# The two mixers' planner: when an item may reserve, when a bank counts as free, and new planned lengths for gate, convolution and memory

## The chip, the cores and the metric

The kernel runs on one core of a Trainium2 chip. The metric is the device time of one execution in microseconds; the time before is the median of three executions. A core has a matrix engine (PE, with its weight loads shown apart as PEld), a vector engine (DVE), a scalar engine (ACT), a general engine (POOL) and a queue engine (SP). SP and POOL start the transfers. Each engine works through its instructions in the order in which they were written for it, and waits where an instruction needs something that isn't there yet.

## The reference, cut to what matters

It is a two-layer encoder over 512 tokens of width 1024, all in f32, with a memory of 256 tokens:

```python
for layer in range(2):
    xn = rms_norm(x, mix_norm[layer])
    if layer == 0:
        mixed = fox_diff_mixer(xn, ...)     # 8 forgetting heads + 4 differential heads
    else:
        mixed = mlstm_mixer(xn, ...)        # 4 heads, chunkwise in the reference
    x = x + mixed
    x = x + memory_cross_attention(rms_norm(x, ...), rms_norm(mem, ...), wq, wkv, wo)
    x = x + conv_ffn(rms_norm(x, ...), ...)
return rms_norm(x, final_norm)
```

The first mixer projects the normed x to fq, fk, fv (forgetting attention, head width 64) and dq, dk, dv (differential attention). A forgetting head adds a decay that depends on the distance to the scores, a differential head subtracts one softmax from another (`p1 - lam * p2`) and norms its output; the two results stand side by side before the output product with `w_out`. The second mixer convolves q and k over four tokens, applies SiLU, weighs the scores with gates i and f, divides by a sum, norms each head, multiplies by sigmoid(og) and goes through its output product.

## The kernel before, in words

Activations lie transposed in SBUF: eight tiles x0 to x7 of 128 channels by 512 tokens. An f32 product is made of three passes of a faster format: each operand is split into a high and a low part, and `mm3` (lines 340 to 342) issues high by high, low by high, high by low into one PSUM bank. Weights come as 128x1024 tiles `raw` over SP; ACT casts the high part `wh`, DVE subtracts it to give the low part `wl`. There are three buffers each of raw, wh and wl, so at most three weight tiles are in use at once. A product over 1024 channels is 24 matmuls of 512 columns, or 24 of 256 columns where the 256 memory tokens are multiplied (xk0 to xk3 below). Line 262 is the helper that issues every ACT and DVE instruction, so those rows of the profile are told apart by the tile names.

PSUM has four banks "acc" for products, two "s" for scores and norms, two "w" for transposes and weighted sums.

The stages, by the trace: first mixer 0 to about 225 us, its memory attention to about 335, its feed-forward to about 700, second mixer to about 935, then memory attention, feed-forward and the last norm. Within the two mixers (and the memory attention) a small planner, `Plan`, decides the order in which the instructions are written. The code adds items: `take` and `free` name resources (banks, buffers), `dur` is the time on PE, `chain` lists what follows on A (ACT), D (DVE) or as a plain delay ("-"), `prio` ranks, `after` is an earliest planned time, `order` and `deps` are items that must come first. `Plan.run` keeps a planned clock t, goes through the items by rank and issues the first whose time has come; the item's function then writes its instructions. An item of higher rank that is not yet due reserves its resources (`held`), so that items of lower rank that want the same are passed over. `pick.ready` is t after the chain: items that depend on it wait until then in the plan. A low-ranked group of products stands ready as fill: in the first mixer the keys of the memory (xk) and the output product (wo).

Names in the first mixer: `x0` to `x7` also hold softmax rows while their x lies in DRAM, and are loaded again before the residual add. A differential head is weighed by line 793 (`pt` transposed probabilities, `v` values), squared into `tb`, summed by the matmul of line 499, made into `z` on DVE, into `y` on POOL, sent by POOL to DRAM (`roots`), and brought back spread over all partitions (`hrb`); DVE then scales `ta` by hrb and splits it to `mh` and `ml`. For a forgetting head, POOL brings the decays (`fb`) and makes a masked bias `tb` from them, which DVE adds to the scores (lines 750 and 751, transposes 781). A pair of forgetting heads is weighed by line 1008. `tb` has two buffers for both uses.

Names in the second mixer: mqk0 to mqk7 are the products of q (0 to 3) and k (4 to 7), mv the values, mog the output gates. `gates` makes the rows of i and f; `ucols` (line 1630) transposes them to columns; `most` and `emts` spread rows by matmul (line 690) for head 0, `both` by DMA for the others. `score` is line 1721, `dens` lines 1743 and 1744; num and hrb are the numerators and the spread norm of a head.

Of the kernel before, what the change touches and what calls it, by code (L numbers as in the profile page):

```python
# [30 lines left out]
ROW_DMA, SPREAD_DMA, LATE = 2.7, 6.0, 12.0  # L31
# [50 lines left out]


class Plan:

# [9 lines left out]

    def add(self, fn, dur=0.0, deps=(), prio=None, take=(), free=(), chain=(), pre=(), after=0.0, order=(), load=(), st=None):
        it = Item(fn, dur, [d for d in deps if d is not None], len(self.items) if prio is None else prio, take, free, chain, pre, after, order, load, st)
        it.n = len(self.items)
        self.items.append(it)
        return it  # L100

    def run(self):
        todo = sorted(self.items, key=lambda i: (i.prio, i.n))
        eng, t = self.eng, self.t
        while todo:
            soon, pick = float("inf"), None
            held = set()
            for i in todo:
                if any(d.ready is None for d in i.deps + i.order) or held & set(i.take):
                    continue  # L110
                held |= set(i.take)
                if any(len(self.res[r]) < i.take.count(r) for r in i.take):
                    continue
                at = max([i.after] + [d.ready for d in i.deps] + [sorted(self.res[r])[i.take.count(r) - 1] for r in i.take])
                if at <= t:
                    pick = i
                    break
                soon = min(soon, at)
# [14 lines left out]
            t += pick.dur  # L133
            u = t + (0.1 if pick.chain else 0.0)
            for e, d in pick.chain:
                if e == "-":
                    u += d
                    continue
                u = max(u, eng[e]) + d
                eng[e] = u  # L140
                u += 0.06
            for e, d in pick.load:
                eng[e] = max(eng[e], t) + d
            pick.ready = u
            pick.fn()
            for r in pick.free:
                if r == "acc":
                    self.banks[pick.st["banks"].pop(0)] = u
                else:
                    self.res[r].append(u)  # L150
# [138 lines left out]
class Builder:  # L289
# [64 lines left out]
    def p_proj(self, pl, src, xs, evac, chain, deps=(), kdeps=None, edeps=(), prio=None, n=SEQ, nk=KB8, order=None, etake=(), per=2, eorder=(), load=()):  # L354
# [5 lines left out]
        for c, e in zip(cuts, cuts[1:] + [nk]):  # L360
# [18 lines left out]
            )  # L379
        return pl.add(lambda: evac(st["ps"]), 0, [last, *edeps], prio, take=etake, free=("acc",), chain=chain, order=eorder, load=load, st=st)  # L380

# [648 lines left out]
    def p_memory(self, pl, layer, at, step, order=()):  # L1030
# [14 lines left out]
        for c in range(2):  # L1045
            last = pl.add(lambda c=c: load(c), 0, (), 0, after=at + step * c - 10.0, order=[*order, last])
        done = {}
# [552 lines left out]
    def mix1(self):  # L1600
        nc, t, tc = self.nc, self.t, self.tc
        H = 4
        with tc.tile_pool(name="mix1", bufs=1, reuse_waits="tile") as mp:
# [382 lines left out]
```

## Time and profile before

| what | value |
|---|---|
| median of three executions | 1425.62 us (1424.94 to 1427.39) |
| the profiled execution | 1423.48 us |
| its span in the trace | 1421.7 us |
| mean granted PE clock | 0.998 |
| PE busy | 1403.3 us, 99% |
| DVE busy | 1133.5 us, 80% |
| ACT busy | 823.8 us, 58% |
| POOL busy | 129.9 us, 9% |

Between the span and the time of the execution lie 1.8 us. PE is busy in 99% of the span: what a change of order alone can win is the rest, and any time in which PE runs at less than its pace. The view of waits says what PE waited for, the table of windows says in which stage; a time in a window is to be read against the window's length.

### The profile page before, as it was taken

Reading aid. Unit: us, or ns where it says so; the run is one execution under the profiler, and the core shown is the slowest. Engines: PE = TensorE matmul, PEld = TensorE weight load, DVE = VectorE, ACT = ScalarE, POOL = GpSimd, SP = SyncE. Lnnn points to the kernel's source line nnn. Section 1 sums busy time; section 2 is a strip of 40 time slices with the busy share of each in tenths; the row PEclk is TensorE's granted clock in tenths of the full one; section 3 lists DMA queues with packets and bytes.
Section 4 is the critical chain, followed back from the end, with each engine's and each line's share of the span. In section 5 each row is a group of like instructions: output and inputs, shape, how many; then the busy total and the mean of one; then the engine's idle time right before and its main releaser. Section 6 shows DMA issues by size and latency. Waiting matters only on the chain.

```text
span 1421.7 us, 22241 instructions
## 1 busy us (share of the span) xinstructions
PE 1403.3 (99%) x8440; PEld 1262.9 (89%) x8440; DVE 1133.5 (80%) x1906; ACT 823.8 (58%) x1382; POOL 129.9 (9%) x189
## 2 busy tenths in 40 slices
PE   9999999999999999999999999999999999999998
PEld 7878788899889999999887788989988999999997
DVE  7778596666689999999768657667667999999984
ACT  7777574444476656566456654445445665656655
POOL 0001240000001111110001210000000111111000
PEclk9999999999999999999999999999999999999999
DMA  5233224323248777773233322323323886777522
GB/s 205 90 108 108 90 79 152 132 76 133 86 150 217 191 180 184 182 182 106 86 105 112 105 95 97 119 92 120 130 74 120 212 202 171 193 179 185 143 77 80
DMA packets 69211, 190.02 MB, mean 134 GB/s; under 512 B 7552, under 2 KB 7552, under 8 KB 69104
## 3 DMA queue, kind: packets, MB, share of 16 engines
q1 hardware_dynamic: 55648, 153.48, 32.3%
q0 software_dynamic: 12448, 34.00, 13.7%
q8 instruction: 66, 1.08, 0.3%
q10 hardware_dynamic: 1008, 1.12, 0.2%
q14 instruction: 41, 0.34, 0.1%
HBM read 186.43 MB, written 2.15 MB: 133 GB/s over the span
## 4 chain that ended last, share of the span: by engine, by line
PE 83%; DVE 8%; ACT 4%; issue 3%; DMA 1%; POOL 1%; SPq 0%; POOLq 0%; DVEq 0%; ACTq 0%
PE acc L340 16%; PE acc L341 16%; PE acc L342 16%; PE w L340 5%; PE w L342 5%; PE w L341 5%; PE s L340 3%; PE s L341 3%; PE s L342 3%; PE acc L402 2%; PE acc L404 2%; PE acc L403 2%; DVE wl L262 2%; DVE x L262 1%; PE w L1765 1%
## 5 line engine op out<-in xcount | busy, mean ns | idle before, releaser
L262 ACT CAST wh<-raw 128x1024 fp32r<-128x1024 f32 (+2 forms) x229 | 235.0, 1027 | 205.6 <-PE acc L341 118.8
L262 DVE TENSOR_TENSOR wl<-raw,wh 128x1024 fp32r<-128x1024 f32 (+2 forms) x229 | 274.2, 1198 | 38.7 <-ACT wh L262 38.2
L340 PE MATMUL acc<-xh,wh 128*128 128x512 f32 (+1 forms) x800 | 278.6, 348 | 0.8 <-ACT v L262 0.8
L341 PE MATMUL acc<-xl,wh 128*128 128x512 f32 (+1 forms) x800 | 274.0, 343 | 0.0
L342 PE MATMUL acc<-xh,wl 128*128 128x512 f32 (+1 forms) x800 | 273.6, 342 | 0.0
L340 PEld LDWEIGHTS acc<-xh,wh 128*128 128x128 f32 x800 | 152.5, 191 | 14.5 <-ACT v L262 1.2
L342 PEld LDWEIGHTS acc<-xh,wl 128*128 128x128 f32 x800 | 152.4, 190 | 13.9
L341 PEld LDWEIGHTS acc<-xl,wh 128*128 128x128 f32 x800 | 152.5, 191 | 13.2
L262 DVE SCALAR_TENSOR_TENSOR c<-hs,vec,c 128x512 f32<-128x512 f32 x176 | 131.8, 749 | 3.8 <-ACT c L262 0.8
L340 PE MATMUL w<-ah,wh 128*128 128x512 f32 x304 | 115.7, 381 | 0.2 <-ACT c L262 0.2
L342 PE MATMUL w<-ah,wl 128*128 128x512 f32 x304 | 115.2, 379 | 0.0
L341 PE MATMUL w<-al,wh 128*128 128x512 f32 x304 | 115.2, 379 | 0.0
L262 ACT ACTIVATE c<-hs,vec 128x512 f32<-128x512 f32 x88 | 70.8, 811 | 9.9 <-DVE hs L262 5.4
L262 ACT CAST ah<-c 128x512 fp32r<-128x512 f32 x44 | 27.2, 619 | 83.8 <-DVE c L262 83.8
L262 DVE TENSOR_TENSOR x<-acc,x 128x512 f32<-128x512 f32 (+1 forms) x43 | 28.1, 653 | 54.2 <-PE acc L342 53.4
L340 PEld LDWEIGHTS w<-ah,wh 128*128 128x128 f32 x304 | 57.6, 190 | 8.0 <-DVE x L262 0.9
L342 PEld LDWEIGHTS w<-ah,wl 128*128 128x128 f32 x304 | 57.5, 189 | 8.1
L341 PEld LDWEIGHTS w<-al,wh 128*128 128x128 f32 x304 | 57.6, 190 | 6.5
L342 PE MATMUL acc<-mem,wl 128*128 128x256 f32 (+1 forms) x192 | 59.9, 312 | 0.0
L340 PE MATMUL acc<-mem,wh 128*128 128x256 f32 (+1 forms) x192 | 59.6, 311 | 0.0
L341 PE MATMUL acc<-mem,wh 128*128 128x256 f32 (+1 forms) x192 | 59.6, 311 | 0.0
L1446 POOL DMA_DIRECT2D sa<-in_up_dram x36 | 30.8, 857 | 290.6 <-DMA sa<-in_up_dram 212.7
(357 smaller groups left out, 3750.5 us busy)
## 6 DMA issues: line engine op xcount, KB each, us to landing
raw<-in_up_dram SPq DMA_DIRECT2D x52, 512.0 KB, 3.7
sa<-in_up_dram SPq DMA_DIRECT2D x36, 512.0 KB, 3.4
sa<-in_up_dram POOLq DMA_DIRECT2D x36, 512.0 KB, 5.9
raw<-in_down_dram SPq DMA_DIRECT2D x32, 512.0 KB, 3.6
ra<-in_up_dram SPq DMA_DIRECT2D x36, 256.0 KB, 4.0
sb<-in_up_dram POOLq DMA_DIRECT2D x36, 256.0 KB, 4.9
raw<-in_xk_dram SPq DMA_DIRECT2D x16, 512.0 KB, 3.2
raw<-in_wo_dram SPq DMA_DIRECT2D x16, 512.0 KB, 3.3
```

The costliest lines, as they stand in the source:

```text
L262: i = issue(*a, **k)
L340: mm(out, wh, xh, start=first, stop=False, skip_group_check=parts)
L341: mm(out, wh, xl, start=False, stop=False, skip_group_check=parts)
L342: mm(out, wl, xh, start=False, stop=last, skip_group_check=parts)
L402: mm(ps, xh[k][:, ts], wh, start=(k == 0), stop=False)
L403: mm(ps, xh[k][:, ts], wl, start=False, stop=False)
L404: mm(ps, xl[k][:, ts], wh, start=False, stop=(k == 7))
L1446: return add("POOL", 0.0029 * cols, lambda: nc.gpsimd.dma_start(out(), src(), accum_op=ALU.add), deps, due, (), (), 6.0)
L1765: nc.tensor.matmul(ps[:, lo:], vv[s][:, c], a[:], start=(s == 0), stop=(s == 3))
```

## The change

Five things change, none of them in what is computed; the numbers of matmuls, transposes, splits and transfers stay the same.

- A constant `HOLD = 2.5`: an item that is known to be due more than 2.5 us later than the planned clock no longer reserves what it takes, so that lower-ranked items may use it meanwhile.
- The PSUM bank of a channel-major product (`p_proj`) counts as free after the first step of the chain that reads it, where it counted as free at the chain's end (`soon=True`).
- The two transfers of the memory are planned 16 us ahead of their use, 10 before.
- In the second mixer the chain from the gates to `ucols` is a delay of 14 us with loads of 5 on ACT and 7 on DVE (it was 1.0, 7.0 and 0.5 in sequence), the chain to `gk` one of 4 us with loads, `most` and `emts` of head 0 also depend on `gk`, and `both` counts two transfers one after the other.
- The planned chain of the convolution, `cc`, is longer (ACT 0.7, 0.6, 0.6 for 0.52 each, DVE 2.3 for 1.98).

```diff
+HOLD = 2.5
     def add(...):
-        it.n = len(self.items)
+        it.n, it.soon = len(self.items), soon
...
-                held |= set(i.take)
                 if any(len(self.res[r]) < i.take.count(r) for r in i.take):
+                    held |= set(i.take)
                     continue
                 at = max([i.after] + [d.ready for d in i.deps] + [sorted(self.res[r])[i.take.count(r) - 1] for r in i.take])
+                if at < t + HOLD:
+                    held |= set(i.take)
                 if at <= t:
                     pick = i
                     break
...
             u = t + (0.1 if pick.chain else 0.0)
+            clear = None
             for e, d in pick.chain:
...
                 u = max(u, eng[e]) + d
                 eng[e] = u
                 u += 0.06
+                clear = clear or u
...
                 if r == "acc":
-                    self.banks[pick.st["banks"].pop(0)] = u
+                    self.banks[pick.st["banks"].pop(0)] = clear if pick.soon else u
...
-        return pl.add(lambda: evac(st["ps"]), 0, [last, *edeps], prio, take=etake, free=("acc",), chain=chain, order=eorder, load=load, st=st)
+        return pl.add(lambda: evac(st["ps"]), 0, [last, *edeps], prio, take=etake, free=("acc",), chain=chain, order=eorder, load=load, st=st, soon=True)
...
-            last = pl.add(lambda c=c: load(c), 0, (), 0, after=at + step * c - 10.0, order=[*order, last])
+            last = pl.add(lambda c=c: load(c), 0, (), 0, after=at + step * c - 16.0, order=[*order, last])
...
-            g = pl.add(lambda: None, 0, [g], 1, chain=(("A", 1.0), ("D", 7.0), ("A", 0.5)))
-            gk = pl.add(lambda: None, 0, [g], 2, chain=(("-", ROW_DMA),))
+            g = pl.add(lambda: None, 0, [g], 1, chain=(("-", 14.0),), load=(("A", 5.0), ("D", 7.0)))
+            gk = pl.add(lambda: None, 0, [g], 2, chain=(("-", 4.0),), load=(("A", 2.4), ("D", 1.2)))
...
-            cc = (("D", 0.6), ("A", 0.52), ("D", 1.98), ("A", 0.52), ("D", 0.66), ("A", 0.52))
+            cc = (("D", 0.6), ("A", 0.7), ("D", 2.3), ("A", 0.6), ("D", 0.66), ("A", 0.6))
...
-                    b1 = pl.add(most, MM, [uc, qe], p, take=("s",), free=("s",), chain=(("A", 0.5),))
-                    b2 = pl.add(emts, MM, [uc, qe], p + 1, take=("s",), free=("s",), chain=(("A", 0.5),))
+                    b1 = pl.add(most, MM, [uc, gk, qe], p, take=("s",), free=("s",), chain=(("A", 0.5),))
+                    b2 = pl.add(emts, MM, [uc, gk, qe], p + 1, take=("s",), free=("s",), chain=(("A", 0.5),))
                 else:
-                    b1 = b2 = pl.add(both, 0, [uc, gk, *turn[-1:]], p, chain=(("-", SPREAD_DMA),))
+                    b1 = b2 = pl.add(both, 0, [uc, gk, *turn[-1:]], p, chain=(("-", ROW_DMA), ("-", SPREAD_DMA)))
```

The order changes in the two mixers alone: PE's first 329 rows, the memory attentions and the feed-forwards stand as they stood. In the listings below the helper's line is 262 before and 269 after; all lines behind the first edit move by 7.

In the first mixer, the differential heads' norms are issued earlier against the softmax of the forgetting heads. On DVE before, in the softmax of the first pair of forgetting heads (ISA rows add the bias `tb` to scores `s`), the scaling of head 2 by `hrb` stands between two blocks:

```order
L262 TENSOR_SCALAR x_140<-x_140,sm_1507 128x384
L262 COPY pt_1370<-w_1543 128x128
L262 ISA x_142,sm_1557<-s_1550,tb_1551 128x384
L262 ISA sm_1557 128x1
L262 SCALAR_TENSOR_TENSOR ta_1421<-ta_1421,warm,hrb_1568 128x512
L262 ISA x_138,sm_1566<-s_1559,tb_1560 128x512
L262 ISA sm_1566 128x1
L262 RECIPROCAL sm_1557<-sm_1557 128x1
L262 TENSOR_TENSOR ml_135<-ta_1421,mh_129 128x512
```

In the new order the scaling of the same head (`hrb_1400`) stands behind the pair's last block and the splits of kb, 52 rows behind its `z`, where it stood 12 rows behind it:

```order
L269 ISA x_143,sm_1558<-s_1551,tb_1552 128x512
L269 ISA sm_1558 128x1
L269 ISA x_144,sm_1569<-s_1562,tb_1563 128x512
L269 ISA sm_1569 128x1
L269 COPY pt_1408<-w_1571 128x128
L269 COPY pt_1409<-w_1574 128x128
L269 TENSOR_TENSOR kb_115<-tmp_1577,ka_320_1579 64x512
L269 TENSOR_TENSOR kb_117<-tmp_1577,ka_321_1583 64x512
L269 SCALAR_TENSOR_TENSOR ta_1265<-ta_1265,warm,hrb_1400 128x512
L269 TENSOR_SCALAR x_142<-x_142,sm_1499 128x384
```

On POOL, the transfer that brings this hrb stood right behind its roots:

```order
L986 AFFINE_SELECT tb_1501<-fb_1215 128x384
L507 TENSOR_TENSOR y_1486<-z_1485,power 128x4
L448 DMA roots_1532<-y_1486 128x4
L452 DMA hrb_1568<-roots_1532 128x512
L986 AFFINE_SELECT tb_1551<-fb_1217 128x384
L986 AFFINE_SELECT tb_1560<-fb_1215 128x512
```

and now stands behind all eight masks of the pair and the next `fb`:

```order
L455 DMA roots_1363<-y_1324 128x4
L459 DMA hrb_1349<-roots_1327 128x512
L993 AFFINE_SELECT tb_1436<-fb_1312 128x256
L993 AFFINE_SELECT tb_1445<-fb_1314 128x256
L993 AFFINE_SELECT tb_1484<-fb_1312 128x384
L993 AFFINE_SELECT tb_1493<-fb_1314 128x384
L993 AFFINE_SELECT tb_1552<-fb_1312 128x512
L993 AFFINE_SELECT tb_1563<-fb_1314 128x512
L702 DMA fb_1627<-decays_1162 128x512
L459 DMA hrb_1400<-roots_1363 128x512
```

With it, all of head 0's norm comes before the forgetting heads' values; fq0 begins ahead of fv; the scores of differential heads 2 and 3 are written close together among the last of fq0 and the first of fv, and heads 2 and 3 are weighed in the middle of fv3, where they stood in fv2.

At the end of the first mixer, PE before wrote the last weighing (line 1008) with products of the other blocks of wo00 and wo01 around it; xk0 to xk3 had been written among the softmax of the second and third pairs:

```order
L1008 MATMUL w_2425<-pt_2109,v_1213 64x128
L1008 MATMUL w_2425<-pt_2213,v_1213 64x128
L342 MATMUL acc_518_2489<-mh_129,wl_2485 128x512
L340 MATMUL acc_518_2489<-mh_130,wh_2484 128x512
L341 MATMUL acc_518_2489<-ml_136,wh_2484 128x512
L342 MATMUL acc_518_2489<-mh_130,wl_2485 128x512
L340 MATMUL acc_514_2456<-qa_509_2434,wh_2451 128x512
L340 MATMUL acc_518_2489<-mh_125,wh_2484 128x512
L341 MATMUL acc_518_2489<-ml_131,wh_2484 128x512
L341 MATMUL acc_514_2456<-qa_510_2435,wh_2451 128x512
```

Now wo00, wo01 and wo02 are begun among those softmaxes and held until the last weighing, and xk0 follows behind them:

```order
L1015 MATMUL w_2399<-pt_2164,v_1310 64x128
L1015 MATMUL w_2399<-pt_2324,v_1310 64x128
L347 MATMUL acc_375_1843<-qa_507_2408,wh_1838 128x512
L347 MATMUL acc_386_1881<-qa_507_2408,wh_1876 128x512
L347 MATMUL acc_443_2073<-qa_507_2408,wh_2068 128x512
L348 MATMUL acc_375_1843<-qa_508_2409,wh_1838 128x512
L349 MATMUL acc_375_1843<-qa_507_2408,wl_1839 128x512
L348 MATMUL acc_386_1881<-qa_508_2409,wh_1876 128x512
L349 MATMUL acc_386_1881<-qa_507_2408,wl_1877 128x512
L348 MATMUL acc_443_2073<-qa_508_2409,wh_2068 128x512
L349 MATMUL acc_443_2073<-qa_507_2408,wl_2069 128x512
L347 MATMUL acc_512_2421<-mem_1518,wh_2416 128x256
```

What moved: four products of 24 matmuls of 256 columns went from before the last weighing to behind it, and 34 more matmuls of wo (63 for 29) from behind it to before it.

In the second mixer, PE before wrote `ucols` right behind the values (mv), ahead of mqk0:

```order
L403 MATMUL acc_1465_7884<-wl_8038,xh_1452_7835 128x512
L404 MATMUL acc_1465_7884<-wh_8037,xl_1453_7836 128x512
L1630 MATMUL s_8074<-ident,cv_7961 128x4 x4
L340 MATMUL acc_1508_8087<-xh_1415_7636,wh_8082 128x512
L341 MATMUL acc_1508_8087<-xl_1416_7637,wh_8082 128x512
L342 MATMUL acc_1508_8087<-xh_1415_7636,wl_8083 128x512
```

Now 21 of mqk0's 24 matmuls come first:

```order
L347 MATMUL acc_1506_8080<-xh_1449_7818,wh_8075 128x512
L348 MATMUL acc_1506_8080<-xl_1450_7819,wh_8075 128x512
L349 MATMUL acc_1506_8080<-xh_1449_7818,wl_8076 128x512
L1637 MATMUL s_8102<-ident,cv_7961 128x4 x4
L347 MATMUL acc_1506_8080<-xh_1452_7835,wh_8075 128x512
L348 MATMUL acc_1506_8080<-xl_1453_7836,wh_8075 128x512
```

Behind it, the spreading of `most` and the first scores move back by six matmuls each, and at the last head the order is `at3`, twelve matmuls of mog, lines 1743 and 1744, where 24 stood between.

More of the change, by code (lines that the diff above doesn't have):

```diff
@@ L94, in __init__, with add @@
         self.res["acc"] = self.banks.values()
-    def add(self, fn, dur=0.0, deps=(), prio=None, take=(), free=(), chain=(), pre=(), after=0.0, order=(), load=(), st=None):
+    def add(self, fn, dur=0.0, deps=(), prio=None, take=(), free=(), chain=(), pre=(), after=0.0, order=(), load=(), st=None, soon=False):
         it = Item(fn, dur, [d for d in deps if d is not None], len(self.items) if prio is None else prio, take, free, chain, pre, after, order, load, st)
-        it.n = len(self.items)
+        it.n, it.soon = len(self.items), soon
         self.items.append(it)
```

## The prediction

> **What bounds the kernel now.** I read the page's busy shares first, then the table of windows over the two mixers, the view of waits, and the timeline around each wait.
>
> ```profile
> PE 1403.3 (99%) x8440; PEld 1262.9 (89%) x8440; DVE 1133.5 (80%) x1906; ACT 823.8 (58%) x1382; POOL 129.9 (9%) x189
> ```
>
> PE is the bound. Of the span of 1421.7 us it is idle for 18.4. The change only reorders two stages, so what counts is their share of that idle time, and any time at less than full clock. In the windows below, the columns are the stretch, its length, then each engine's busy time; the last three are PE's granted clock, the transfers' share and GB/s.
>
> ```profile
> 75.00:100.00 25.00, 24.30 (x119) 20.68 (x118) 20.19 (x60) 17.93 (x40) 2.39 (x4) 1.00 0.36 114
> 100.00:125.00 25.00, 24.01 (x130) 20.45 (x129) 16.77 (x53) 20.45 (x47) 4.97 (x8) 1.00 0.26 84
> 150.00:160.00 10.00, 7.50 (x34) 6.41 (x33) 6.43 (x17) 5.04 (x12) 5.19 (x8) 0.83 0.29 78
> 180.00:200.00 20.00, 18.55 (x136) 16.02 (x136) 19.21 (x65) 15.86 (x39) 9.11 (x15) 1.00 0.19 63
> 740.00:760.00 20.00, 18.53 (x89) 15.97 (x88) 13.63 (x18) 14.87 (x19) 1.13 (x2) 1.00 0.25 79
> 760.00:780.00 20.00, 19.06 (x87) 15.86 (x86) 17.80 (x26) 12.65 (x22) 4.64 (x10) 1.00 0.39 124
> 780.00:800.00 20.00, 19.15 (x83) 14.59 (x82) 14.63 (x29) 12.98 (x22) 5.18 (x9) 1.00 0.49 154
> 850.00:900.00 50.00, 49.69 (x271) 42.76 (x270) 35.77 (x57) 23.16 (x33) 4.45 (x7) 1.00 0.27 90
> ```
>
> So the first mixer loses 0.70 + 0.99 in 75 to 125, 2.50 (with a low clock besides) in 150 to 160, and 1.45 in 180 to 200, where DVE is busy 19.21 of 20: there DVE, not PE, sets the pace. The second loses 1.47 + 0.94 + 0.85 + 0.31. That is 9.2 us and the clock: the change can't win more than about 11 us. PE's longest waits in 75 to 235 us (in all, times, longest) name who ends them:
>
> ```profile
> PE w L781 <- DVE pt L262: 2.5, 1, 2.5
> PE w L793 <- ACT pt L262: 1.0, 1, 1.0
> PE w L781 <- DVE sm L262: 0.9, 1, 0.9
> ```
>
> **First term: the scaling of head 2, -4.2 us.** The longest wait, from the timeline:
>
> ```profile
> 151.11 0.56 POOL L695 DMA_DIRECT2D fb<-decays  x1 [0.30 <-POOL tb L986]
> ...
> 152.19 0.75 DVE L262 SCALAR_TENSOR_TENSOR ta<-ta,warm,hrb 128x512 f32<-128x512 f32 x1 [2.06 <-DMA hrb<-roots]
> ...
> 153.63 0.69 DVE L262 TENSOR_TENSOR ml<-ta,mh 128x512 fp32r<-128x512 f32 x1
> ...
> 154.24 0.77 DVE L262 TENSOR_SCALAR x<-x,sm 128x384 f32<-128x384 f32 x1
> ...
> 155.26 0.69 PE L781 MATMUL w<-ident,x 128*128 128x128 f32 x2 [2.50 <-DVE pt L262]
> ...
> 157.02 0.63 PE L341 MATMUL acc<-xl,wh 128*128 128x512 f32 x1
> 157.45 0.63 PE L342 MATMUL acc<-xh,wl 128*128 128x512 f32 x1
> ...
> 158.72 0.38 PE L342 MATMUL acc<-xh,wl 128*128 128x512 f32 x1
> 158.93 0.38 PE L340 MATMUL acc<-xh,wh 128*128 128x512 f32 x1
> ```
>
> DVE, in order, stands 2.06 us before the spread norm; behind it stand the copy of pt that frees the "w" bank, and PE's transposes behind that: 2.50 us. Then matmuls start 0.43 us apart until 158.72 and 0.21 apart from there (0.216 is used for a 512-column matmul below): 3.46 us at half pace, 1.7 lost. The price of this place is 2.5 + 1.7 = 4.2. The Trainium skill (TensorE: Matmul & The Clock Gate, Part 1) says that the array falls to half its clock after an idle window of about 3.4 us. Here 2.50 us, right behind sums of two columns, was enough, so the measurement decides; by the page's length alone the place would cost 2.5 and the forecast be 1.7 us later.
>
> In the new order this scaling stands behind both last blocks of the pair. Is its hrb there? POOL now issues it behind the pair's last mask, which needs the second-last pair of blocks read, since `tb` has two buffers.
>
> ```profile
> hrb<-roots POOLq DMA_DIRECT2D x7, 256.0 KB, 3.6
> ```
>
> ```profile
> L262 DVE CUSTOM_DVE_ANT_0 x<-s,tb 128x512 f32<-128x512 f32 (+3 forms) x27 | 13.2, 498 | 3.1 <-PE s L751 1.5 <-POOL tb L986 1.3
> L262 DVE TENSOR_TENSOR kb<-tmp,ka 64x512 fp32r<-64x512 f32 x4 | 2.8, 706 | 0.1
> L262 DVE SCALAR_TENSOR_TENSOR ta<-ta,warm,hrb 128x512 f32<-128x512 f32 x2 | 1.5, 749 | 2.1 <-DMA hrb<-roots 2.1
> L262 DVE TENSOR_TENSOR ml<-ta,mh 128x512 fp32r<-128x512 f32 x2 | 1.4, 685 | 0.0
> ```
>
> From that read: a mask of about 0.6 (estimated by the 512-column passes here), 0.30 and 0.56 for fb, then 3.6 to land: some 5.1 us. On DVE meanwhile stand one scaling (0.75), one ml (0.69), one evacuation of the same size (0.69), two kb (1.41), two full-width score blocks (about 0.7 each), and ten short rows (about 1.5): 6.4. So 1.3 us to spare: I take no wait; the other end is the whole 4.2 again. Heads 0, 1 and 3 have 13 us or more of DVE work between z and hrb (their rows summed by such durations), for a path that took head 2 no more than 9.
>
> **Second term: heads 2 and 3 packed, +0.3.** Their 16 score blocks now stand among 47 product matmuls (10.2 us) with 32 score matmuls (5.0) and the transposes (1.3): 16.5 us of PE. DVE's rows for them, from 81 to 122 us before:
>
> ```profile
> L262 DVE CUSTOM_DVE_ANT_0 x<-s,dmask 128x512 f32<-128x512 f32 (+3 forms) x17 | 8.3, 496 | 3.1 <-PE s L751 3.1
> L262 DVE TENSOR_TENSOR wl<-raw,wh 128x1024 fp32r<-128x1024 f32 x5 | 6.0, 1208 | 0.8 <-ACT wh L262 0.8
> L262 DVE SCALAR_TENSOR_TENSOR x<-x,sm,x 128x512 f32<-128x512 f32 (+3 forms) x8 | 4.3, 542 | 1.9 <-ACT x L262 1.8
> ```
>
> 16 x 0.496 + 8 x 0.542 + 4 x 1.208 = 17.1, with some 7.5 for the reciprocals, the copies of pt, the qa and ta that stand between (an estimate by their sizes): 24.6 us. In DVE's queue a row begins before the last one's end (ml above ends at 154.32, the next begins at 154.24): 0.08 each over 71 rows, 5.7 less, some 19 to 20. PE may run two blocks ahead (two "s" banks), about 1.5 us of DVE, and the end of DVE's work falls beside fv1 to fv3, which need none of it. 20 - 1.5 - 16.5 = 2.0 lost, where 1.69 was. The waits of 0.9 and 1.0 (L781 for sm, L793 for pt) go with the old order, since the weighings now stand 10 us behind the scores. Ends for the loss: 0, and 8.1 (no overlap, nothing hidden).
>
> **Third term: the end of the first mixer, +2.2.** The fill among the softmaxes shrinks by 96 x 0.108 (256 columns) - 34 x 0.216 = 3.0 us, and DVE has three splits fewer to make there (3.6 us). They balance. What is new stands behind the last weighing:
>
> ```profile
> 218.44 2.37 PE L1008 MATMUL w<-pt,v 128*64 128x512 f32 x16
> ...
> 220.88 0.59 ACT L262 CAST qa<-w 128x512 fp32r<-128x512 f32 x1 [2.51 <-PE w L1008]
> ...
> 221.51 0.69 DVE L262 TENSOR_TENSOR qa<-w,qa 128x512 fp32r<-128x512 f32 x1 [2.81 <-ACT qa L262]
> ...
> 222.77 1.06 ACT L262 CAST wh<-raw 128x1024 fp32r<-128x1024 f32 x1 [1.30 <-PE acc L341]
> ```
>
> Before, products of other blocks covered the cast of 0.59 and the split of 0.69. Now PE has nothing between: 0.65 lost, then three matmuls (0.65) cover the split. wo00, wo01, wo02 hold all three weight buffers until 1.75, 2.2 and 2.6 us after the weighing. xk0's cast can't start before the first of these: it ends at 3.0 (0.4 lost), and its low part, on DVE behind two residual adds of about 0.7, at 4.5; PE has two matmuls first and loses 1.3. Before the weighing itself, the last block takes about 4.4 us through DVE, ACT, PE and DVE, and PE has 3.8 of work: 0.6. With 0.7 for the masks (POOL now sends head 3's hrb between two of them) it is 3.65, for 1.45 before. Ends: no more than before (DVE is relieved more than the fill shrinks, and xk's parts come in time) and 6.65 (the 3.0 us of missing fill shown whole).
>
> **Fourth term: the second mixer, -1.65.**
>
> ```profile
> 750.68 0.38 PE L1630 MATMUL s<-ident,cv 4*128 4x4 f32 x4 [1.47 <-DVE cv L262]
> ...
> 770.09 0.61 ACT L262 ACTIVATE k<-cv 128x512 f32<-128x512 f32 x1
> 770.75 1.77 PE L1721 MATMUL s<-q,k 128*128 128x512 f32 x4 [0.94 <-ACT k L262]
> ...
> 784.39 1.77 PE L1721 MATMUL s<-q,k 128*128 128x512 f32 x4 [0.85 <-ACT k L262]
> ...
> 860.73 0.75 DVE L262 SCALAR_TENSOR_TENSOR num<-num,vec,hrb 128x512 f32<-128x512 f32 x1 [1.16 <-DMA hrb<-roots]
> ...
> 881.42 0.91 PE L1744 MATMUL w<-mk,ones 128*128 128x384 f32 x2 [0.32 <-DVE mk L262]
> ```
>
> Behind 21 matmuls (4.5 us) ucols waits for nothing: 1.47 won. But ACT's and DVE's queues up to the first k are the old ones, so k is still there at 770.70 and L1721 still starts near 770.75, now with six more matmuls done: 6 x 0.216 = 1.3 is what remains. At head 1 the memory's rows have moved out of the way of k, and the 0.85 goes (ends: all or nothing). At head 3 only 12 matmuls (2.6 us) stand between the last score and L1744, for 24 before, and the scaling by head 2's hrb, which already waited 1.16 us, stands ahead of the sum on DVE: 0.8 for 0.32, +0.5 (ends -0.3 and +1.5). -1.3 - 0.85 + 0.5 = -1.65.
>
> **At nothing.** The memory's earlier transfers: no row of PE waits for them; each holds one of the three raw buffers 6 us longer, and two still carry the stream, as a product of 24 matmuls lasts 5.2 us and loading, cast and split take less than twice that. Banks counted free early: PE still waits for the true read, and no wait of PE on "acc" stands in the list of 75 to 235 us. The larger cc only moves rows.
>
> Sum: -4.2 + 0.3 + 2.2 - 1.65 = -3.35. The profiled execution goes from 1423.48 to 1420.1; the median of 1425.62 is 2.1 above that execution, so 1422.3. A difference of 0.2% (2.85 us) is about what can be told from none.
>
> **Rivals.**
> - The end of the first mixer costs nothing new, because three splits fewer on a DVE that is busy 19.21 of 20 free more than the fill lost: 3.35 + 2.2 = 5.5 won, 1420.1. For it: DVE's share there. Against: the three held buffers.
> - The wait for hrb only moves: head 2's lands after DVE gets there, or head 3's holds up the masks. 2.5 to 4.2 come back: 1424.8 to 1426.5. The spare 1.3 us decides.
> - Slower: the packed heads wait row by row. If each row of DVE waits for ACT's answer, durations add without overlap: 8.1 lost for 1.69, +2.75 in all, 1428.4. The change is slower by more than 0.2% once the stretch loses over 8.2. For it: DVE waited 1.8 us for ACT ahead of its eight combinations there, with more work between them than now.
> - Slower, by the clock alone: short pauses, each under a microsecond, halve PE's pace for much of the 16.5 us; five drops by 1.7 make +8.5 and 1430.8. The window 180 to 200, with 1.45 us of such pauses at a clock of 1.00, speaks against it. This is what the Trainium skill's page TensorE: Matmul & The Clock Gate describes under "A second HAM failure mode: psum-queue depth-cycling"; by that rule the clock would swing here, and this trace doesn't show it.
>
> **How the numbers follow.** Forecast 0.42 (its own range 1419.5 to 1425: 0.27 faster, 0.15 same); first rival 0.17, faster; second 0.17 (0.01 faster, 0.12 same, 0.04 slower, with the end of the mixer at its bad end); third 0.19 (0.04 same, 0.15 slower, since it would delay the heads' norms too); fourth 0.05, slower. Together faster 0.45, same 0.31, slower 0.24. The range runs from the first rival with the packed heads' loss at 0 (1418.1), the second mixer's last head at its good end (1417.3) and 0.8 of the spread between runs (1416.5) to the third with 0.6 of spread (1429).
>
> **What would show it.** In the profile after: PEclk 1.00 throughout the first mixer and no wait of L781 beyond 1 us for pt around 150 us; PE idle about 2 us in the packed stretch (some 80 to 100 us); about 2.4 us of idle in front of xk0, with waits on a cast and on wl; no wait at L1630, one of about 1.3 at the first L1721, none at the second, and about 0.8 at L1744 of the last head. A low clock anywhere in 75 to 230, or a DVE wait for hrb of over 2 us, would make the forecast wrong.

## The result, and the profile after

The changed kernel takes 1428.88 us (median of 18 runs, 1425.31 to 1432.15), the kernel before beside it 1424.96 (18 runs, 1423.66 to 1428.08). The ratio is 1.0026, with a 95% interval of 1.0018 to 1.0034: slower by 0.26%, 3.9 us. The forecast was 1422.3. The time lies at the upper end of its range (1429.0), on the side that had the smallest chance (0.24).

The profiled execution of after took 1431.04 us, with a span of 1429.3. The number of instructions is the same; PE's busy time grew by 4.1 us, its idle time by 3.5. The two profiled executions lie 7.6 us apart, the medians 3.9: the profile of before is one of its quicker executions, that of after one of its slower, so the two profiles show more loss than the medians.

```profile
PE 1407.4 (98%) x8440; PEld 1265.0 (89%) x8440; DVE 1133.3 (79%) x1906; ACT 823.1 (58%) x1382; POOL 129.2 (9%) x189
```

The table of windows of after, as in the prediction (stretch, length, busy times, then PE's granted clock, the transfers' share and GB/s):

```profile
75.00:100.00 25.00, 24.64 (x130) 20.32 (x128) 21.47 (x74) 23.40 (x57) 2.35 (x3) 1.00 0.18 54
100.00:125.00 25.00, 22.93 (x110) 19.01 (x109) 17.71 (x45) 16.84 (x33) 2.42 (x5) 1.00 0.40 138
125.00:150.00 25.00, 24.28 (x117) 21.29 (x118) 18.43 (x49) 18.65 (x40) 9.08 (x15) 0.93 0.35 102
150.00:175.00 25.00, 25.00 (x131) 21.67 (x130) 19.39 (x42) 15.27 (x28) 1.38 (x4) 1.00 0.32 109
175.00:200.00 25.00, 21.75 (x121) 16.24 (x121) 19.57 (x67) 14.96 (x40) 12.53 (x21) 0.93 0.24 64
200.00:225.00 25.00, 22.55 (x132) 17.23 (x131) 17.56 (x57) 13.45 (x32) 3.51 (x7) 1.00 0.28 86
740.00:760.00 20.00, 20.00 (x95) 17.27 (x95) 14.12 (x20) 13.09 (x18) 0.59 (x1) 1.00 0.24 80
850.00:900.00 50.00, 48.09 (x219) 39.08 (x218) 26.34 (x40) 24.12 (x35) 4.50 (x6) 0.97 0.25 80
```

The same windows of before, where the prediction showed other cuts:

```profile
125.00:150.00 25.00, 24.87 (x124) 20.56 (x123) 21.64 (x52) 20.07 (x39) 5.06 (x7) 1.00 0.34 110
150.00:175.00 25.00, 22.50 (x111) 19.37 (x109) 15.46 (x34) 11.52 (x22) 6.15 (x10) 0.93 0.32 100
175.00:200.00 25.00, 23.55 (x172) 19.66 (x172) 21.19 (x70) 17.63 (x42) 10.19 (x17) 1.00 0.16 55
200.00:225.00 25.00, 24.91 (x155) 19.66 (x154) 20.78 (x66) 14.15 (x37) 4.10 (x9) 1.00 0.51 173
```

The stretch of the first term (150 to 175) is what was promised: PE is busy all of it at full clock, where it lost 2.50 us and 7% of the clock. But two stretches that ran at full clock now don't (125 to 150 and 175 to 200), and 100 to 125, 175 to 200 and 200 to 225 lose 2.07, 3.25 and 2.45 us. From 75 to 225 PE's idle time is 8.85 us where it was 5.86, and the clock costs 2 x 0.07 x 25 = 3.5 where it cost 1.75: 4.7 more.

The view of waits of after begins with these (in all, times, longest); the first two aren't in the list of before, and the third was 0.32 there:

```profile
PE w L788 <- DVE x L269: 2.4, 1, 2.4
PE w L788 <- ACT ta L269: 2.0, 1, 2.0
PE w L1751 <- DVE mk L269: 1.9, 1, 1.9
```

**A, at 125 us: a row of the memory's on ACT.** The timeline of after:

```profile
116.84 1.22 DVE L269 TENSOR_TENSOR wl<-raw,wh 128x1024 fp32r<-128x1024 f32 x1
...
118.08 0.33 SPq L1049 DMA_DIRECT2D raw<-in_mem_dram  x1
118.50 0.38 SPq L332 DMA_DIRECT2D raw<-in_fq_dram  x1
...
124.07 0.42 ACT L269 ACTIVATE sqt<-raw 128x256 f32<-128x256 f32 x1 [5.08 <-DMA raw<-in_mem_dram]
...
124.39 0.57 ACT L269 COPY ta<-w 128x512 f32<-128x512 f32 x1
...
125.01 0.55 PE L788 MATMUL w<-ident,x 128*128 128x128 f32 x3 [2.03 <-ACT ta L269]
...
126.27 1.05 PE L506 MATMUL s<-ones,tb 128*128 128x2 f32 x8 [0.70 <-ACT tb L269]
```

The first square of the second memory tile stands on ACT one row ahead of the copy of `ta` (the weighed values of differential head 2) that frees a "w" bank. Heads are counted from 0 here, as with the scaling of head 2; the packed "heads 2 and 3" of the prediction are heads 1 and 2 in this count. The tile that the square reads is issued at 118.08, although planned earlier: it needs one of the three raw buffers, and `wl` on DVE gives one back at 118.06. The tile is there at 124.07, ACT stands 5.08 us, and PE 2.03 and 0.70 behind it; then the clock drops.

**B, at 190 us: the fill is used up.** PE has no product left while DVE splits `qa` and `kb`. **C, at 887 us:** the sum of the last head stands on DVE behind the scaling by head 2's `hrb`. B and C in the timeline:

```profile
187.40 0.90 DVE L269 TENSOR_TENSOR kb<-tmp,ka 64x512 fp32r<-64x512 f32 x1
188.31 0.69 DVE L269 TENSOR_TENSOR qa<-tmp,qa 64x512 fp32r<-64x512 f32 x1
189.01 0.69 DVE L269 TENSOR_TENSOR kb<-tmp,ka 64x512 fp32r<-64x512 f32 x1
...
190.85 0.66 PE L788 MATMUL w<-ident,x 128*128 128x128 f32 x4 [2.45 <-DVE x L269]
...
192.34 1.09 PE L788 MATMUL w<-ident,x 128*128 128x128 f32 x4 [0.47 <-DVE sm L269]
...
885.17 0.75 DVE L269 SCALAR_TENSOR_TENSOR num<-num,vec,hrb 128x512 f32<-128x512 f32 x1 [2.79 <-DMA hrb<-roots]
...
887.04 0.91 PE L1751 MATMUL w<-mk,ones 128*128 128x384 f32 x2 [1.91 <-DVE mk L269]
```

To compare runs by stage, the table of experiments gives two lengths from each profiled execution: "first" runs from the start to the first transpose of the memory attention's probabilities (line 1201 of before), "second" from the last matmul of the gate product (line 637) to the first of the last group of four such transposes. Before, the starts stand in these rows (min, median and max duration, first and last start; the last group of four begins 0.33 us ahead of the last start):

```profile
L1201 PE MATMUL w<-ident,xe x64: 272/273/273, 282.9 to 1048.4; 128*128 128x128 f32 x64
```

```profile
L637 PE MATMUL w<-xh,wh x16: 379/379/379, 6.7 to 726.6; 128*40 128x512 f32 x8, 128*100 128x512 f32 x8
```

### The profile page after: what moved, and what is told of

It is laid out like the page before. It is cut to its first block, busy times and chain, and to the rows that moved or that the text cites. A ratio compares the mean times of both kernels' runs of the same rounds, so it can differ in the third digit from the quotient of the medians.

```text
span 1429.3 us, 22252 instructions
## 1 busy us (share of the span) xinstructions
PE 1407.4 (98%) x8440; PEld 1265.0 (89%) x8440; DVE 1133.3 (79%) x1906; ACT 823.1 (58%) x1382; POOL 129.2 (9%) x189
## 3 DMA queue, kind: packets, MB, share of 16 engines
q10 hardware_dynamic: 1008, 1.12, 0.2%
## 4 chain that ended last, share of the span: by engine, by line
PE 83%; DVE 8%; ACT 3%; issue 2%; DMA 2%; POOL 1%; SPq 0%; POOLq 0%; DVEq 0%; ACTq 0%
PE acc L347 17%; PE acc L349 16%; PE acc L348 16%; PE w L347 5%; PE w L349 5%; PE w L348 5%; PE s L347 3%; PE s L349 3%; PE s L348 3%; PE acc L409 2%; PE acc L410 2%; PE acc L411 2%; DVE wl L269 2%; DVE c L269 1%; PE w L1772 1%
## 5 line engine op out<-in xcount | busy, mean ns | idle before, releaser
L349 PEld LDWEIGHTS acc<-xh,wl 128*128 128x128 f32 x800 | 152.8, 191 | 14.0
```

Source lines behind the costliest of these rows:

```text
L349: mm(out, wl, xh, start=False, stop=last, skip_group_check=parts)
```

## The experiments

| kernel | median us (runs) | ratio to before, 95% | first | second |
|---|---|---|---|---|
| before | 1424.96 (18) | | 282.90 | 321.47 |
| after | 1428.88 (18) | 1.0026 (1.0018 to 1.0034) | 287.40 | 323.97 |
| after again | 1428.97 (7) | 1.0040 (1.0025 to 1.0055) | 286.12 | 322.02 |
| first mixer new, second old | 1429.74 (10) | 1.0037 (1.0023 to 1.0050) | 285.25 | 321.73 |
| first mixer old, second new | 1424.27 (11) | 0.9999 (0.9991 to 1.0008) | 282.79 | 324.14 |
| after, sum first | 1429.44 (5) | 1.0032 (1.0020 to 1.0044) | 289.34 | 320.08 |
| after, memory's lead 10 | 1422.20 (11) | 0.9992 (0.9983 to 1.0000) | 279.88 | 321.84 |
| after, fill from 180 | 1426.49 (12) | 1.0023 (1.0014 to 1.0032) | 284.29 | 322.23 |
| first mixer old, second new, sum first | 1422.75 (11) | 0.9997 (0.9988 to 1.0005) | 283.17 | 320.09 |
| after, one row of ACT moved | 1423.04 (11) | 0.9998 (0.9989 to 1.0007) | 281.50 | 321.89 |
| before, memory's lead 16 | 1420.10 (11) | 0.9976 (0.9968 to 0.9985) | 278.95 | 321.55 |
| all three mended | 1418.77 (6) | 0.9969 (0.9958 to 0.9981) | 279.10 | 320.04 |
| all three, again | 1418.83 (5) | 0.9965 (0.9953 to 0.9978) | 278.85 | 320.19 |

The kernel before, run beside each batch, had medians of 1423.6 to 1425.0, so kernels of different batches are compared by ratio.

### Which mixer

The changed kernel once more, unaltered:

> The changed kernel once more, unaltered, as the measure for the runs beside it and to see whether its losses are the same in a second profile. Theory: the changed kernel loses at three new waits (2.03 + 0.70 us at 125, 2.45 + 0.47 us at 190, 1.91 us at 887 in its first profile), and PE's clock falls behind each of them, for some 1.5 to 1.75 us each. The waits are set by the order and should be there again within 0.3 us; whether the clock falls may differ from execution to execution, and would make the spread of its times (1425.3 to 1432.2) wider than that of the kernel before. Rival: the waits themselves come and go with the transfers; then another profile shows other waits.

It was slower again. Its profiled execution (1427.22) has the wait B unaltered, 1.04 us in place of A's 2.03, and 1.79 at C with no drop of the clock. So A and C vary between executions; B's wait doesn't.

Next, a flag puts one mixer's plan back to the old one:

```diff
-    def __init__(self, prev=None, hold=(), **res):
+    def __init__(self, prev=None, hold=(), new=True, **res):
+        self.new, self.hold_t = new, HOLD if new else 1e9
...
-                if at < t + HOLD:
+                if at < t + self.hold_t:
...
-        return pl.add(lambda: evac(st["ps"]), ..., st=st, soon=True)
+        return pl.add(lambda: evac(st["ps"]), ..., st=st, soon=pl.new)
...
-            last = pl.add(lambda c=c: load(c), 0, (), 0, after=at + step * c - 16.0, order=[*order, last])
+            last = pl.add(lambda c=c: load(c), 0, (), 0, after=at + step * c - (16.0 if pl.new else 10.0), order=[*order, last])
```

With `new=False` for the first mixer:

> The first mixer in the order of the kernel before, the second mixer in the changed order. Theory (both mixers lose): the second mixer won 1.47 + 0.85 and lost 1.91, 0.66, 0.51, 0.21 more at the first score and 1.5 us of clock: +0.5 to +2.0 us against the kernel before, 1425.5 to 1427. Rival (the prediction's fourth term holds, all the loss is in the first mixer): -1.65, 1423.3.

With `new=False` for the second, and its chains (`g`, `gk`, `cc`, `most`, `emts`, `both`) as before:

> The first mixer in the changed order, the second in that of the kernel before. Theory: the wait of 2.50 at 153 is gone with its clock loss, the waits at 125 and 190 and 2.0 us at the end of the mixer have come, two with clock loss: +2.5 to +4.3 us against the kernel before, 1427.5 to 1429.3. Rival (all the loss is in the first mixer): +5.5, 1430.5. The two splits should add up to the changed kernel's difference.

The loss is the first mixer's: with it old the time is that of before (0.9999; its theory was a loss of 0.5 to 2 us), with the second old the loss stays (1.0037, some 5.3 us, close to the 5.5 of its rival). The second mixer's new plan gave nothing either: in these two profiles of it the second stretch is 0.5 and 2.7 us longer than before (322.02 and 324.14), the latter with a pause of 1.94 us at C and a lower clock behind it.

The profile with the second mixer old has A at its mildest. There the tile was on hand 3.7 us after its issue, no wait for `ta` is left, and PE pauses for a single 0.66 us; the clock falls all the same (in this kernel all lines stand one further on than in after):

```profile
121.88 0.42 ACT L270 ACTIVATE sqt<-raw 128x256 f32<-128x256 f32 x1 [2.83 <-DMA raw<-in_mem_dram]
...
124.08 1.05 PE L507 MATMUL s<-ones,tb 128*128 128x2 f32 x8 [0.66 <-ACT tb L270]
```

```profile
125.00:128.00 3.00, 3.00 (x12) 2.55 (x12) 0.98 (x2) 3.00 (x7) 2.09 (x4) 0.52 0.01 1
```

### Three places

First C alone. The scalings of head 2 by `hrb` go behind the last head's last score and its sum; four rows of DVE change their place:

```diff
+                    if h == 3:
+                        self.sumlast = i.ins.name
...
+                if h == 3:
+                    scale2.order.append(se)
...
+                        if h == 2:
+                            nc.vector.last = self.sumlast
+                            nc.vector.follow()
...
+                    scale2 = f
```

> The changed kernel with one thing moved: at the last head of the second mixer, DVE's two scalings by the spread norm of head 2 stand behind the head's last score and sum, not ahead of them. Theory: DVE's wait of 2.79 us for the transfer no longer stands before the sum, PE's wait of 1.91 at line 1751 falls under 0.4, and the clock loss behind it (1.5) goes: -1.5 to -3.4 us against the changed kernel. Rival: the scaled head's products wait in its place and the time stays within 0.5 us.

Its window of 850 to 900 has no idle time left:

```profile
850.00:900.00 50.00, 50.00 (x248) 41.54 (x247) 29.41 (x44) 27.09 (x39) 5.42 (x7) 1.00 0.27 91
```

The second stretch falls to 320.08, 1.4 us below before and 1.9 to 3.9 below after. The total doesn't show it, since A was at its worst in this profile: 1.41 + 0.70 us of waits and a clock of 0.86 in 125 to 150, a first stretch of 289.34. The same edit beside the old first mixer, where A can't be, gave 320.09:

> The first mixer in the order of the kernel before, the second in the changed order with the sum of the last head ahead of the scalings. Theory: the second mixer's change is worth -1.4 us against the kernel before once its new wait is out (320.1 for 321.5 in the stage's length): 1422.5. Rival (the gain of the single profile is noise of the stage): within 0.5 of the kernel before.

There too the total moved by less than the interval can tell (0.9997 against 0.9999 without the edit); the gain of 1.4 us is shown by the stage, in two profiles, and not by a median.

Then the memory's transfers of the first mixer, planned 10 us ahead again:

```diff
-            last = pl.add(lambda c=c: load(c), 0, (), 0, after=at + step * c - 16.0, order=[*order, last])
+            last = pl.add(lambda c=c: load(c), 0, (), 0, after=at + step * c - (10.0 if layer == 0 else 16.0), order=[*order, last])
```

> The changed kernel with the first mixer's memory transfers planned 10 us ahead again (16 in the second mixer, as changed); on ACT the squares of the second memory tile then stand behind both copies of ta. Theory: the wait at 125 us (1.04 and 2.03 for ta in two profiles, with 0.7 for tb) comes from ACT standing before that tile's transfer, and it is what makes the times spread from 1425 to 1433: the ta wait goes, the first mixer (to the first score of the memory attention) falls from 286.1 to 287.4 to about 284, the median by 3 to 4 us, and the spread halves. Rival (the tile comes when a weight buffer comes free, and the wait passes to the next reader): first mixer unchanged within 0.5.

This one line is more than the whole loss, and more than was expected of it: 1422.20, ratio 0.9992, and ten of its eleven runs lie between 1421.1 and 1422.6, where after spreads over nearly 8 us. PE has no wait at 125 and the clock is 1.00 from 75 to 225. But the line changes more than A: from 147 us on PE's order is another, though xk0 still stands behind the last weighing, and B has become 0.70:

```profile
186.34 1.06 PE L788 MATMUL w<-ident,x 128*128 128x128 f32 x8 [0.70 <-DVE x L269]
```

And the fill: the start of the fill in the first mixer moved from 210 to 180 in the plan, so that products remain for the softmax of the last pairs:

```diff
-FILLS, FILL_AT, FILL_PRIO = 2, (210.0, 140.0), 99
+FILLS, FILL_AT, FILL_PRIO = 2, (180.0, 140.0), 99
```

> The changed kernel with the fill (xk0 to xk3) planned from 180 instead of 210 in the first mixer, so that it stands among the softmaxes again and wo00 alone is held. Theory: with HOLD the fill lost its place to wo00 to wo02, and the waits at 190 (2.45 + 0.47, with 1.75 of clock) and behind the last weighing (0.68 + 1.10) come from that: 4 to 6 us less in the first mixer, with the wait at 125 still there and as variable as before. Rival (DVE sets the pace there whatever PE is given): the waits move to other softmax blocks, less than 1.5 us won.

B goes from 2.45 to 0.68, with no drop of the clock there, and a wait of 1.04 for `sm` comes in at 218.82 instead. The first stretch shrinks to 284.29, 1.8 to 3.1 us less than the two profiles of after, where 4 to 6 less was expected; A is still in it (1.64 + 0.70, clock 0.93), and the ratio of 1.0023 can't be told from that of after.

### One row, and the lead alone

Is it the early transfer that costs, or the one row of ACT behind it? After, with this row tied behind the copy of `ta`, everything of SP, PE and POOL in its place; on DVE the one add that reads the square goes back with it:

```diff
-                    nc.scalar.copy(o["o"][:], ps[:])
+                    self.tacopy = getattr(self, "tacopy", []) + [nc.scalar.copy(o["o"][:], ps[:]).ins.name]
...
+                    if k == 4:
+                        self.nc.scalar.last = self.tacopy[2]
+                        self.nc.scalar.follow()
                     self.squares(k, raw, MEM, state)
+                    if k == 4:
+                        self.nc.scalar.follow()
```

> The changed kernel with one row of ACT moved: the first square of the second memory tile (sqt<-raw) stands behind the copy ta<-w of the third differential head, where it stood one row ahead of it. The memory's transfers keep their lead of 16 us and every other row of SP, PE and POOL its place. Theory (this one row, waiting in ACT's queue for a transfer that lands late, is the whole price of the memory's lead): no wait of PE for ta near 125 us, PEclk 1.00 in 125 to 150, the first mixer (to the first score of the memory's attention) about 280 us as with the lead undone (279.9), and the time about 1422 to 1423. Rival (the early transfer itself costs, by holding a raw buffer and sharing the engines with fq's weights): the first mixer stays at 284 or more and the time at 1426 or more, with waits for weights. Rival (it is the pile of short rows there that lowers the clock): the wait goes but 125 to 150 stays at 0.93, and the first mixer lies near 282 to 284.

The row is it. The tile is issued at the same place and there 5.0 us later (5.9 in after), but nothing that PE waits for stands behind its square:

```profile
118.22 0.33 SPq L1049 DMA_DIRECT2D raw<-in_mem_dram  x1
118.64 0.38 SPq L332 DMA_DIRECT2D raw<-in_fq_dram  x1
...
119.55 0.59 ACT L269 COPY ta<-w 128x512 f32<-128x512 f32 x1 [0.43 <-PE w L800]
...
122.97 0.53 PE L788 MATMUL w<-ident,x 128*128 128x128 f32 x3
...
125.19 0.42 ACT L269 ACTIVATE sqt<-raw 128x256 f32<-128x256 f32 x1
```

Its windows show the stretch whole, and B's wait unaltered, this time without a fall of the clock:

```profile
100.00:125.00 25.00, 24.94 (x127) 20.97 (x127) 18.66 (x49) 21.21 (x39) 3.59 (x7) 1.00 0.41 138
125.00:150.00 25.00, 25.00 (x121) 21.78 (x121) 21.31 (x57) 18.08 (x41) 8.63 (x15) 1.00 0.45 127
175.00:200.00 25.00, 21.75 (x127) 17.24 (x125) 23.85 (x85) 18.39 (x52) 12.59 (x22) 1.00 0.16 44
```

This one row of ACT, with its reader on DVE, takes the ratio from 1.0026 and 1.0040 to 0.9998, 4 to 6 us. The times spread over 2.9 us in its eleven runs, where after spreads over nearly 8. Both waits of PE at A were ended by ACT and none by DVE, but the two rows were not moved one without the other. That holding the buffer or sharing the engines costs by itself is refuted, and so is the thought that the short rows there lower the clock without a wait. The forecast of 280 for the first stretch was missed by 1.5: with the lead undone the order of the end came out different too, and B is 0.70 there for 2.45 + 0.47 here.

Then the lead of 16 in the kernel before, nothing else changed:

```diff
-            last = pl.add(lambda c=c: load(c), 0, (), 0, after=at + step * c - 10.0, order=[*order, last])
+            last = pl.add(lambda c=c: load(c), 0, (), 0, after=at + step * c - (16.0 if layer == 0 else 10.0), order=[*order, last])
```

> The kernel before with one part of the change alone: the memory's transfers of the first mixer planned 16 us ahead, 10 before; all else old. PE's order differs in 42 rows. Theory (the lead costs only where the order puts a memory row of ACT just ahead of a copy that PE waits for): in the old order no copy of ta follows at once behind such a row, so the first mixer stays within 1 us of the 282.9 of before, the wait near 153 us for hrb included, and the time within 1.5 us of before (ratio 0.999 to 1.001). Rival (the lead costs by itself): the first mixer 2 to 7 us longer, ratio 1.0015 to 1.005, with a new wait of ACT for raw<-in_mem that PE shows too.

Both were wrong: it is faster, by 0.24% (0.15 to 0.32). In the timeline of before, ACT waits for the first memory tile too, and rows of it stand ahead of the copies that PE waits for at 104:

```profile
98.53 0.42 ACT L262 ACTIVATE sq<-raw 128x256 f32<-128x256 f32 x1 [2.91 <-DMA raw<-in_mem_dram]
...
103.00 0.49 ACT L262 ACTIVATE mem<-raw,vec 128x256 fp32r<-128x256 f32 x1
103.39 0.56 ACT L262 COPY ta<-w 128x512 f32<-128x512 f32 x1
103.86 0.47 ACT L262 COPY pt<-w 128x384 f32<-128x384 f32 x1
...
104.38 1.99 PE L793 MATMUL w<-pt,v 128*128 128x512 f32 x5 [0.99 <-ACT pt L262]
```

The tile, issued at 92.27 before, is now issued at 90.45; ACT doesn't wait for it, its rows are done by 97.7, and the copy comes 2.8 us sooner:

```profile
97.15 0.50 ACT L262 ACTIVATE mem<-raw,vec 128x256 fp32r<-128x256 f32 x1
...
101.03 0.48 ACT L262 COPY pt<-w 128x384 f32<-128x384 f32 x1
...
156.74 0.44 PE L781 MATMUL w<-ident,x 128*128 128x128 f32 x2 [1.31 <-DVE pt L262]
```

The 0.99 is gone, the wait of 2.50 near 153 is 1.31, and the clock is 1.00 in 150 to 175: 0.99 + 1.19 + 1.75 = 3.9, which is what the first stretch lost (282.90 to 278.95). Only the 0.99 goes with the tile. Between 150 and 163 us PE's order came out different too, so that PE has work until 155.4 where it stopped at 152.8; DVE still stands behind hrb there, for 2.40 us. Why the plan came out so isn't tested.

### All three mended

The lead of 10, the fill from 180 and the sum first, in one kernel, twice:

> The changed kernel with all three: memory planned 10 us ahead in the first mixer, fill from 180, the sum of the second mixer's last head ahead of the scalings. Theory: the three causes are separate and add: first mixer some 279 us, second about 320 (from its first gate product to the last score of the memory attention), 1417 to 1420 in all, faster than the kernel before by 4 to 6. Rival: orders interact, and one of the waits returns elsewhere: 1422 to 1426.

> The version with the three places mended, once more beside these two: the memory's lead of the first mixer back at 10, the fill of the first mixer from 180 instead of 210, the sum of the last head ahead of the scaling. Theory: 1418 to 1420, ratio 0.9958 to 0.998, first mixer 279 to 280, second 320. If its gain was luck of one batch, the ratio goes to 0.999 or above.

At 1418.8 it beats both kernels, before by 0.31% and 0.35%. Its windows from 175 on show what is left, 1.24 and 1.63 us at the end of the first mixer:

```profile
175.00:200.00 25.00, 23.76 (x175) 20.80 (x175) 20.62 (x58) 16.14 (x37) 8.00 (x14) 1.00 0.37 117
200.00:225.00 25.00, 23.37 (x128) 16.93 (x127) 18.87 (x60) 14.76 (x36) 3.82 (x8) 1.00 0.31 101
850.00:900.00 50.00, 50.00 (x276) 42.45 (x275) 31.77 (x49) 24.62 (x34) 5.58 (x7) 1.00 0.29 99
```

## Why the prediction was wrong

**"At nothing": the memory's earlier transfers. This step failed, and it made the kernel slower.** It asked who waits for the transfer on PE, and whether buffers suffice. It didn't ask what the rows that use the tile stand in front of: a square that nobody waits for, one row ahead of a copy that PE waits for. The step also took a transfer planned earlier as one issued earlier; it was issued when a buffer came free, at 118 (118.08 for 119.15 before; the first tile 90.14 for 92.27). Price: 2.03 + 0.70 and the clock in the profile of after, 1.04 + 0.70 and the clock in the second; moving the one row brought 4 to 6 us back. That leaves the time of before (0.9998), not the gain that was forecast; the rest of the forecast was lost in the third and fourth terms.

**First term, -4.2: right.** The wait at 153 is gone and the clock with it, 2.50 + 1.75. The sum behind it was close: instead of 1.3 us to spare, DVE waits 0.19 us for hrb at 152.27; PE doesn't show it.

**Second term, +0.3: too high.** The stretch of 75 to 100 loses 0.36 us, and outside A nothing is lost in 100 to 125 (24.94 of 25 with the row moved). So heads 2 and 3 packed cost about 0.4, where 2.0 was forecast and 1.69 was lost before: -1.3. The waits at A carry ACT's name, but have nothing to do with the third rival's row by row.

**Third term, +2.2: the sentence "They balance" failed at one place.** The fill that shrank by 3.0 us was set against 3.6 us of splits on DVE, two sums over a stretch of 40 us. But four splits of qa and kb stand together at 186 to 190, and the 23 matmuls of xk2 that ran beside such splits before were gone: 2.45 + 0.47 at one place, and 1.75 for the clock. The other parts came as forecast or lower: 0.68 for the cast (0.65), 1.10 for xk0's low part (0.4 + 1.3). In all 175 to 225 loses 5.70 + 1.75, against 1.54 before: +5.9. The sums themselves held elsewhere: with the lead undone and the same shrunken fill the stretch loses 3.76 us at full clock, which is the forecast +2.2. So the order at B cost the rest, and either of two edits, the fill from 180 or the other order with the lead undone, takes it out.

**Fourth term, -1.65: two of four parts.** The wait for ucols is gone, and 1.15 for 0.94 at the first score: -1.26 (forecast -1.3; its list of signs says 1.3 for that wait, but its own sum leaves 1.47 + 0.94 - 1.3 = 1.1). The 0.85 at head 1 is gone, but 0.66 for `at` at 795.92 took its place: -0.2. L1744 (now 1751) waits 1.79 to 1.91 for 0.32, the bad end and not the +0.5 taken; the scaling by hrb ahead of the sum was seen, but its wait was taken for the old 1.16, and it was 2.79: POOL now issues that transfer at 881.57, beside the last head's sum, where it stood at 857.06, and DVE is ready for it 0.8 us after the issue instead of 2.5. With the sum first, the stage gains 1.4 of the 1.65.

With the row moved the time is 0.02% below before, with the lead undone 0.08%, both within what can be told from none; with the three mended it is 0.31 to 0.35% below, more than the 0.23% of the forecast. The fourth rival's cause, the clock, was there, though not in the packed stretch: the drops stand behind A, B and C, mostly behind pauses of 1 to 2.5 us, and once, at A, behind a single one of 0.66. The prediction's own test, "a low clock anywhere in 75 to 230", is what showed it wrong.

## What to carry to other kernels

For a transfer that is moved, look up on every engine that works in order which row uses its data, and what stands behind that row: the same six microseconds of planned lead went with 3.6 us gained in one order and with 5 to 7 lost in another, though the transfers were issued only 1 to 2 us earlier. Two amounts of work balance only if they stand beside each other; compare them place by place, not as sums over a stage. A new pause of PE can cost more than its length: most of those near 2 us or above, and some shorter ones, brought some 1.7 us more in these runs. Its length is the one end of its price, the length and 1.7 us the other.

## What the runs showed of the hardware

PE's clock falls after pauses well under 3.4 us, and not at a fixed length. At C, the same place in the same order, pauses of 1.54, 1.69, 1.74 and 1.79 us left it at 1.00, and 1.91 and 1.94 were followed by matmuls 0.43 us apart. In after, the half pace begins at 888.46, 1.4 us after the pause at C has ended at 887.04, and ends 3.4 us on:

```profile
888.46 0.63 PE L347 MATMUL acc<-xh,wh 128*128 128x512 f32 x1
888.88 0.63 PE L348 MATMUL acc<-xl,wh 128*128 128x512 f32 x1
...
891.85 0.38 PE L349 MATMUL acc<-xh,wl 128*128 128x512 f32 x1
```

At B, 2.45 us was followed by a fall in four profiles, and by none in a fifth (the one with the row moved, clock 1.00 in 175 to 200). At A, between groups of eight two-column sums, 1.04 + 0.70 us was enough, and in the profile with the second mixer old 0.66 us alone (clock 0.52 in 125 to 128); with the row moved there was no pause there and no fall. In the first profile with all three mended, 2.13 us ahead of a 256-column matmul at 1130 brought no fall (clock 1.00 in 1128 to 1140). Half clock for about 3.4 us costs 1.7; at A with the sum first it lasted longer (0.86 over 25 us, 3.5 lost). The Trainium skill (TensorE: Matmul & The Clock Gate, Part 1) says that the gate watches a free-running window of about 3.4 us, so that where a transition falls depends on the phase. The four falls and the one miss at B agree with that, though no run here varied the phase by itself; that a whole window of idleness is needed does not agree, at 1.91 us and at 0.66.

The second memory tile, 512 KB issued 0.4 us ahead of a weight tile of the same size, was on hand for ACT 3.7, 5.0, 5.4 and 6.0 us after its issue in four profiled executions of the same first mixer. An order with no slack for that goes with a wide spread: after over nearly 8 us, with the one row moved over 2.9, with all three mended over 2.5.
